# Down's first visits and the reading of its operands: other visit lengths, reads in quarters, two short visits

## The chip, the cores and the metric

The kernel runs on one core of one Trainium2 chip. The metric is the device time of one execution in microseconds; for the kernel before, the median of three runs is given. The core has five engines that this text names: TensorE (PE, with its weight loads PEld), VectorE (DVE), ScalarE (ACT), GpSimd (POOL) and SyncE (SP). Each takes its own instructions in order. Transfers are issued by SP's queue, some by POOL's and ACT's.

## The reference

One layer of an encoder on 512 tokens of width 2048, in float32: two attention mixers side by side, cross attention over 256 memory tokens, an MLP and a last norm. The change touches the MLP's second half and the norm alone:

```
hm = rmsnorm(x, g_mlp[l])
x = x + jnp.square(jax.nn.relu(hm @ w_up[l])) @ w_down[l]
return rmsnorm(x, g_final)
```

`w_up` is 2048 x 8192 and `w_down` 8192 x 2048.

## The kernel before, in words

Activations lie transposed: features on the 128 partitions, the 512 tokens along the columns. Every float32 product is three matmuls: each operand is split into a rounded part (hi) and the rest (lo), by a cast on ACT and a subtract on DVE (`hi_lo`, line 331), and hi x hi, hi x lo and lo x hi are added up in a PSUM bank. There are eight banks.

The MLP multiplies blocks of two by two with seven products in place of eight (`PRODUCTS`, named p1, q6, p7, q4, p2, q5, p3). One **unit** is one such block: a weight block of 256 x 512 against one **pair** of operands. A pair is two tiles of 128 features by 512 tokens, kept as seven sums of 256 columns, 1792 columns of hi and 1792 of lo. A unit (`strassen_pe`, line 1493) is 7 products x 2 halves x 3 matmuls of 256 columns, 42 matmuls, all on line 308.

**Up** is 16 groups `g` of 8 units; the 8 pairs of its input (`XP`) lie in the eight slots of the tile `big`. **Down** has four column groups `ng` of 512 features. Each needs 32 units, one for each of the 32 pairs that Up leaves. As only eight pairs are resident (`TP`, in the same slots of `big`), Down goes in 16 **visits** `v` of 8 units (`down_units`, line 1692): visit `v` takes column group `v % 4` and the pairs `2v` to `2v + 7`, modulo 32. So the window of pairs moves by two from visit to visit, and the pairs 0 to 5 are read a second time for the last three visits (`NLOAD = 38`).

At the end of a group of Up, `gen_up_out` (line 1523) evicts the seven banks, applies relu and square and the norm's factor, forms the seven sums in the buffer `G` (columns 0 to 4095 of the tile `fb`), and stores two pairs to `tp_dram` (line 1581). `gen_load_t` (line 1605) reads a pair back on SP's queue (line 1614, 896 KB in one transfer) and splits it by `hi_lo`. It is called once in each unit of Up's last group, when that unit's slot of `XP` is done with, and after the first two units of a visit, for the slots of the two pairs that the window leaves.

At the end of a visit `gen_down_out` (line 1640) evicts its seven banks with one ACT copy and eleven DVE additions onto `CB[ng]`, which holds the residual and then the sum. It can start when the residual has been read: `gen_load_res` (line 1626), started by the first unit of Down, waits until Up's last group has been stored, since `CB[0]` and `CB[1]` lie where `G` was, and issues 16 reads (line 1635). A unit needs seven banks when its visit begins, one bank is spare, and the others come free as the eviction of the visit before goes on. In the last four visits (`v >= 12`) `gen_square` (line 1713) squares the finished tiles on ACT and adds them up on POOL (on DVE for the last), through the one buffer `ev` that `gen_down_out` also uses. `gen_out` then forms the norm and writes the output.

Weights come in a ring of four buffers. For each unit, `load_blocks` (line 1445) issues three reads on SP (lines 1461, 1463, 1465: 256, 256 and 128 KB) and one accumulating read on POOL (line 1470, 256 KB). `strassen_split` (line 1476) adds two sums on DVE and splits in two pieces, of 1024 and 768 columns.

What sets the order: the program is written out by hand by tasks (Python generators) and a planner that keeps a clock for each engine (`Plan`, line 72). PE's instructions are written in unit order, and between them every task whose due time has come writes its next instructions. So the order of the instructions on each engine, and of the transfers on SP's queue, follows from the planner's estimates, for example that a pair's read takes 2,500 ns on the queue and lands 3,000 ns later (line 1615).

Of the kernel before, what the change touches and what calls it, by code (L numbers as in the profile page):

```python
# [158 lines left out]
def kernel(  # L159
# [20 lines left out]
    nc = tc.nc  # L180
# [1403 lines left out]
    def up_units(g):  # L1584
        st = {}

        def pe(kk):
            def run(i):
                if g == 0 and kk == 0:
                    spawn(gen_rstd_l())  # L1590
                until(lambda: kk in XP)
                if kk == 7:
                    spawn(gen_up_out(g, st), True)
                strassen_pe(i, st, XP[kk], kk == 0, kk == 7)
                if g == 15:
                    spawn(gen_load_t(kk))
            return run

        return [Unit(w_up[g * 8 + kk], 1024, pe(kk)) for kk in range(8)]

    NLOAD = 38

    def gen_load_t(s):

        p = s % 32
        yield plan.clk["pe"]
        while ("t", p // 2) not in flag:
            yield 0  # L1610
        dst = big[:, PAIR * (s % 8) : PAIR * (s % 8) + PAIR]
        hi, lo = dst[:, 0:1792], dst[:, 1792:3584]
        src = lo.bitcast(F32)
        nc.sync.dma_start(src, tp_dram[p])
        plan.issue("dma", 2500.0, [src], [], 3000)
        yield from hi_lo(hi, lo, src)
        TP[s] = dst


    CB_OFF = (0, 2048, 9472, 11520)  # L1620
# [69 lines left out]
    keep = []  # L1690

    def down_units(v):
        ng, st = v % 4, {}
        keep.append(st)

        def pe(j):
            def run(i):
                s = 2 * v + j
                if v == 0 and j == 0:
                    spawn(gen_load_res())  # L1700
                until(lambda: s in TP)
                if j == 7:
                    if v >= 12:
                        spawn(gen_square(ng, st), True)
                    spawn(gen_down_out(ng, st), True)
                strassen_pe(i, st, TP[s], j == 0, j == 7)
                if j < 2 and s + 8 < NLOAD:
                    spawn(gen_load_t(s + 8))
            return run

        return [Unit(w_dn[down_index((2 * v + j) % 32, ng)], 1024, pe(j)) for j in range(8)]

    def gen_square(ng, st):

        order = ((1, 0), (0, 0), (1, 1), (0, 1))
        for m, t in order:
            x = CB[ng][m][t]
            while ("fin", id(st), m, t) not in flag or (ng > 0 and ("sqd", ng - 1) not in flag):
                yield 0
            yield rt(x)  # L1720
            s = (yield from take(ev if ng < 3 else sq_l))[0]
            act.activation(s, x, AF.Square)
            yield rt(s)
            acc = acc_f[:, 256 * t : 256 * t + 256]
            eng = dve if ng == 3 else pool
            if ng == 0 and m == 1:
                eng.tensor_tensor(acc, s[:, 0:256], s[:, 256:512], op=OP.add)
            else:
                for e in range(2):
                    eng.tensor_tensor(acc, acc, s[:, 256 * e : 256 * e + 256], op=OP.add)  # L1730
            if ng < 3:
                ev.put(s)
            flag.add(("sqd", ng, m, t))
        flag.add(("sqd", ng))
        if ng < 3:
            for e in range(2):
                gain_tile(ng, 0, e)
                yield 0
        else:
            spawn(gen_out(), True)  # L1740
# [120 lines left out]
    first_s = len(units)  # L1861
    for g in range(16):
        units.extend(up_units(g))
    for v in range(16):
        units.extend(down_units(v))
    for i, u in enumerate(units):
        u.buf = (i - first_s) % 2 if i >= first_s else (i - first_s) % 3
# [166 lines left out]
```

## Time and profile before

| | |
|---|---|
| median of 3 runs | 2368.63 us (2363.82 to 2376.11) |
| profiled execution | 2371.74 us |
| its span, first to last instruction | 2370.0 us |
| mean granted clock of TensorE | 0.985 |
| PE busy | 2254.0 us, 95% |
| DVE busy | 1678.8 us, 71% |
| ACT busy | 1069.8 us, 45% |
| POOL busy | 394.8 us, 17% |
| moved by transfers | 409.05 MB, mean 173 GB/s |
| pairs read back (line 1614) | 38 of 896 KB |

The profile is one execution. An engine's busy time counts its instructions, not the waits between them. Helpers record the operations of many places under one line: L139 is every operation of ACT, DVE and POOL that the planner knows, L308 every matmul of the MLP. So a group is told by its tiles: `hl` holds the split weights, `big` the pairs, `fb` everything that is float32. Of rows with an engine's order of time, each is a run of like instructions: start, length, engine, what, how many, and in brackets the idle time before it with what ended that.

### The profile page before, as it was taken

How to read it: one execution, taken by the hardware profiler on the slowest of the kernel's cores; microseconds unless marked ns; L12 is line 12 of the kernel's file. 1: busy time of each engine (PE TensorE's matmuls, PEld its weight loads, DVE VectorE, ACT ScalarE, POOL GpSimd, SP SyncE). 2: the span in 40 equal slices, each digit the busy share in tenths (PEclk: the TensorE clock that was granted, in tenths of full speed). 3: DMA queues.
4: the chain of work that ended last, by engine and by line, in shares of the span. 5: the costliest groups of instructions: out<-in, count | busy, mean ns of one | idle time of the engine just before them, and what ended most of it. 6: DMA issues, size and time to landing. Idle time of an engine off the chain costs nothing.

```text
span 2370.0 us, 41508 instructions
## 1 busy us (share of the span) xinstructions
PE 2254.0 (95%) x16024; PEld 2165.4 (91%) x16024; DVE 1678.8 (71%) x2620; ACT 1069.8 (45%) x1487; POOL 394.8 (17%) x482
## 2 busy tenths in 40 slices
PE   8999999999999999899999999997799999999995
PEld 8999999998888887899999999997799999999995
DVE  7678543448734567887777878787578787777886
ACT  6543333345533455544545444455244444444442
POOL 3110100122012102211111111111111111111232
PEclk9999999999999999999999999999899999999997
DMA  5322222231243434778888888889877887878773
GB/s 173 101 85 94 69 78 81 65 107 45 89 169 101 157 126 151 184 200 238 206 235 221 230 236 212 246 223 287 257 211 201 238 218 210 221 197 240 202 193 107
DMA packets 259142, 409.05 MB, mean 173 GB/s; under 512 B 22112, under 2 KB 157296, under 8 KB 258688
## 3 DMA queue, kind: packets, MB, share of 16 engines
q1 hardware_dynamic: 220224, 337.58, 44.0%
q0 software_dynamic: 36944, 67.21, 17.0%
q8 instruction: 125, 2.05, 0.3%
q10 hardware_dynamic: 1776, 1.62, 0.2%
q14 instruction: 73, 0.60, 0.1%
HBM read 368.57 MB, written 37.75 MB: 171 GB/s over the span
## 4 chain that ended last, share of the span: by engine, by line
PE 67%; DVE 14%; DMA 9%; issue 6%; POOL 2%; ACT 1%; SPq 1%; DVEq 0%; POOLq 0%; ACTq 0%
PE bank L308 34%; PE bank L303 31%; DVE fb L139 7%; DVE hl L139 5%; DMA fb<-in_w_up_dram 5%; DMA fb<-in_w_dn_dram 2%; DMA big<-tp_dram 2%; DVE big L139 2%; PE bank L328 2%; POOL fb L139 2%; ACT hl L139 1%; ACT big L139 0%; DMA tp_dram<-fb 0%; SPq L1463 0%; DMA fb<-xs_dram 0%
## 5 line engine op out<-in xcount | busy, mean ns | idle before, releaser
L308 PE MATMUL bank<-big,hl 128*128 128x256 f32 x10752 | 1318.6, 285 | 71.3 <-DVE hl L139 35.7
L308 PEld LDWEIGHTS bank<-big,hl 128*128 128x128 f32 x10752 | 1306.6, 193 | 82.8 <-DVE hl L139 41.6
L139 ACT CAST hl<-fb 128x1024 fp32r<-128x1024 f32 (+4 forms) x699 | 637.7, 928 | 947.6 <-PE bank L308 304.2
L139 DVE TENSOR_TENSOR hl<-fb,hl 128x768 fp32r<-128x768 f32 (+4 forms) x698 | 747.5, 1087 | 401.1 <-ACT hl L139 399.6
L303 PE MATMUL bank<-hl,big 128*128 128x384 f32 (+4 forms) x2916 | 525.1, 330 | 7.4 <-ACT big L139 6.3
L303 PEld LDWEIGHTS bank<-hl,big 128*128 128x128 f32 x2916 | 479.2, 189 | 18.5 <-ACT big L139 6.3
L139 DVE TENSOR_TENSOR fb<-fb 128x256 f32<-128x256 f32 (+3 forms) x779 | 399.2, 525 | 134.9 <-DMA fb<-in_w_up_dram 82.0
L303 PE MATMUL bank<-big,hl 128*128 128x512 f32 (+1 forms) x1192 | 296.1, 390 | 0.0
L139 POOL TENSOR_TENSOR fb<-fb 128x128 f32<-128x128 f32 (+5 forms) x209 | 161.9, 797 | 701.2 <-DVE fb L139 308.3
L303 PEld LDWEIGHTS bank<-big,hl 128*128 128x128 f32 x1192 | 222.2, 188 | 43.3
L1470 POOL DMA_DIRECT2D fb<-in_w_dn_dram x128 | 110.8, 866 | 578.5 <-DMA fb<-in_w_dn_dram 311.6
L1470 POOL DMA_DIRECT2D fb<-in_w_up_dram x128 | 110.9, 866 | 531.7 <-DVE fb L139 185.0
L139 DVE TENSOR_TENSOR fb<-fb,bank 128x512 f32<-128x512 f32 x208 | 139.5, 681 | 9.2 <-PE bank L303 1.3
L139 ACT ACTIVATE fb<-fb 128x512 f32<-128x512 f32 (+2 forms) x144 | 116.7, 814 | 60.6 <-DVE fb L139 38.3
L303 PE MATMUL bank<-big 128*128 128x256 f32 (+2 forms) x534 | 113.3, 327 | 2.1 <-DVE big L139 1.2
L139 DVE TENSOR_TENSOR big<-big 128x1792 fp32r<-128x1792 f32 x38 | 76.9, 2023 | 36.4 <-ACT big L139 36.4
L139 ACT CAST big<-big 128x1792 fp32r<-128x1792 f32 x38 | 64.3, 1692 | 74.6 <-DMA big<-tp_dram 74.4
L303 PEld LDWEIGHTS bank<-big 128*128 128x128 f32 x534 | 87.1, 188 | 10.1 <-DVE big L139 2.5
L139 ACT CAST big<-bank 128x512 fp32r<-128x512 f32 (+2 forms) x119 | 61.2, 540 | 56.1 <-PE bank L328 28.0
L139 DVE TENSOR_TENSOR big<-bank,big 128x512 fp32r<-128x512 f32 (+1 forms) x102 | 62.7, 642 | 25.5 <-ACT big L139 25.4
L328 PE MATMUL bank<-cs,fb 128*128 128x128 f32 x384 | 60.2, 275 | 8.9 <-POOL fb L139 3.6
L328 PEld LDWEIGHTS bank<-cs,fb 128*128 128x128 f32 x384 | 46.3, 140 | 17.2 <-POOL fb L139 5.8
(88 smaller groups left out, 705.8 us busy)
## 6 DMA issues: line engine op xcount, KB each, us to landing
fb<-in_w_up_dram SPq DMA_DIRECT2D x256, 256.0 KB, 4.8
fb<-in_w_dn_dram SPq DMA_DIRECT2D x256, 256.0 KB, 5.0
big<-tp_dram SPq DMA_DIRECT2D x38, 896.0 KB, 8.7
fb<-in_w_up_dram POOLq DMA_DIRECT2D x128, 256.0 KB, 5.9
fb<-in_w_dn_dram POOLq DMA_DIRECT2D x128, 256.0 KB, 5.3
fb<-in_w_in_dram SPq DMA_DIRECT2D x80, 384.0 KB, 3.0
tp_dram<-fb SPq DMA_DIRECT2D x32, 896.0 KB, 9.8
fb<-in_w_out_dram SPq DMA_DIRECT2D x32, 512.0 KB, 3.3
```

The lines of the kernel that those rows point to most:

```text
L139: r = fn(*args, **kw)
L303: nc.tensor.matmul(out, lhsT, rhs, start=start, stop=stop)
L308: nc.tensor.matmul(out, lhsT, rhs, start=start, stop=stop, skip_group_check=True)
L328: nc.tensor.transpose(out, in_, ident)
L1470: nc.gpsimd.dma_start(s31, src[:, 256:768], accum_op=OP.add)
```

## The change

The visits come from a table of column group, first pair and end. The first three take 4, 6 and 8 pairs, twelve of 8 pairs follow, then come visits of 4, 2 and 8 pairs. The four visits that finish a column group are 14 to 17, in the order of the groups 2, 0, 1, 3. Only the pairs 0 and 1 are read twice (34 in all). A pair is read in four transfers of 448 columns, a quarter each, in a sequence that `pace` hands out: two quarters for each unit of Up's last group, of visit 0 and of the first two units of visit 1, then one for each unit. Cast and subtract of a pair come after its fourth quarter. The planner now counts 700 ns on the queue and 6,000 ns to landing for a quarter.

```
                 strassen_pe(i, st, XP[kk], kk == 0, kk == 7)
                 if g == 15:
-                    spawn(gen_load_t(kk))
+                    pace(2)
...
-    NLOAD = 38
-
-    def gen_load_t(s):
+    VISITS = [(0, 0, 4), (1, 0, 6), (2, 0, 8)]
+    VISITS += [(v % 4, 2 * v - 4, 2 * v + 4) for v in range(3, 15)]
+    VISITS += [(0, 28, 32), (1, 30, 32), (3, 26, 34)]
+    FINAL = (14, 15, 16, 17)
+    NLOAD = 34
+    paced = [0]
+
+    def pace(n):
+        for _ in range(n):
+            if paced[0] < 4 * NLOAD:
+                spawn(gen_load_t(*divmod(paced[0], 4)))
+                paced[0] += 1
+
+    def gen_load_t(s, x):
 
         p = s % 32
         yield plan.clk["pe"]
-        while ("t", p // 2) not in flag:
+        while ("t", p // 2) not in flag or (x > 0 and ("tq", s, x - 1) not in flag):
             yield 0
...
-        nc.sync.dma_start(src, tp_dram[p])
-        plan.issue("dma", 2500.0, [src], [], 3000)
-        yield from hi_lo(hi, lo, src)
-        TP[s] = dst
+        c = part(448 * x, 448)
+        nc.sync.dma_start(src[:, c], tp_dram[p][:, c])
+        plan.issue("dma", 700.0, [src[:, c]], [], 6000)
+        flag.add(("tq", s, x))
+        if x == 3:
+            yield from hi_lo(hi, lo, src)
+            TP[s] = dst
...
     def down_units(v):
-        ng, st = v % 4, {}
+        ng, s0, s1 = VISITS[v]
+        st, n = {}, s1 - s0
         keep.append(st)
...
-                s = 2 * v + j
+                s = s0 + j
...
-                if j == 7:
-                    if v >= 12:
-                        spawn(gen_square(ng, st), True)
+                if j == n - 1:
+                    if v in FINAL:
+                        spawn(gen_square(v, ng, st), True)
                     spawn(gen_down_out(ng, st), True)
-                strassen_pe(i, st, TP[s], j == 0, j == 7)
-                if j < 2 and s + 8 < NLOAD:
-                    spawn(gen_load_t(s + 8))
+                strassen_pe(i, st, TP[s], j == 0, j == n - 1)
+                pace(2 if v == 0 or (v == 1 and j < 2) else 1)
             return run
...
-    for v in range(16):
+    for v in range(len(VISITS)):
         units.extend(down_units(v))
```

`gen_square` tests the visit where it tested the column group, so that the squares of visit 14 start the sum and those of 17 go to DVE.

## Rows read from the trace of the kernel before

**Rows 1.** The page, part 2: PE's busy tenths in 40 slices of the span.
```profile
PE   8999999999999999899999999997799999999995
```

**Rows 2.** PE in order of time, the passage from Up to Down.
```profile
1499.79 39.04 PE L308 MATMUL bank<-big,hl 128*128 128x256 f32 x324
...
1699.22 3.92 PE L308 MATMUL bank<-big,hl 128*128 128x256 f32 x20 [15.65 <-DVE fb L139]
```

**Rows 3.** Busy time in stretches: length, PE, PEld, DVE, ACT, POOL, PE clock, transfers, GB/s.
```profile
1540.00:1704.33 164.33, 133.43 (x1040) 130.93 (x1040) 122.86 (x159) 77.33 (x80) 21.64 (x25) 0.93 0.87 255
1704.33:2340.42 636.09, 610.90 (x4996) 604.33 (x4996) 501.01 (x658) 278.04 (x296) 119.00 (x137) 0.99 0.77 208
...
1599.30:1660.10 60.80, 46.77 (x339) 44.94 (x338) 48.40 (x56) 34.24 (x32) 6.92 (x8) 0.92 0.92 288
...
1863.00:1878.30 15.30, 13.79 (x114) 13.48 (x113) 14.28 (x22) 5.33 (x7) 1.73 (x2) 1.00 0.64 153
```

**Rows 4.** Waits from 1587 to 1664: in total, times, longest.
```profile
ACT big L139 <- DMA big<-tp_dram: 23.8, 8, 7.1
```

**Rows 5.** SP's queue in order of time, the passage.
```profile
1560.56 1.37 SPq L1581 DMA_DIRECT2D tp_dram<-fb  x2
...
1602.61 2.19 SPq L1581 DMA_DIRECT2D tp_dram<-fb  x2
1604.89 5.00 SPq L1614 DMA_DIRECT2D big<-tp_dram  x2
...
1662.78 1.98 SPq L1581 DMA_DIRECT2D tp_dram<-fb  x2
1664.81 19.40 SPq L1635 DMA_DIRECT2D fb<-xs_dram  x16
1684.66 0.37 SPq L1461 DMA_DIRECT2D fb<-in_w_dn_dram  x1
```

**Rows 6.** The chain that ended last, behind Up's last store: start, length, what.
```profile
1674.26 0.38 SPq L1635
...
1677.81 6.78 DMA fb<-xs_dram
...
1691.14 6.52 DMA fb<-in_w_dn_dram
```

**Rows 7.** PE in order of time, changes of visit in Down.
```profile
1790.29 39.62 PE L308 MATMUL bank<-big,hl 128*128 128x256 f32 x328 [1.51 <-DVE hl L139]
...
2172.95 41.70 PE L308 MATMUL bank<-big,hl 128*128 128x256 f32 x344 [1.24 <-DVE fb L139]
2217.14 41.12 PE L308 MATMUL bank<-big,hl 128*128 128x256 f32 x328 [2.50 <-DVE hl L139]
```

**Rows 8.** Groups by shape, 1900 to 2370: count, busy us, mean ns, idle before.
```profile
L139 DVE TENSOR_TENSOR hl<-fb,hl 128x1024 fp32r<-128x1024 f32 x81 | 101.0, 1247 | 42.5 <-ACT hl L139 41.7 <-PE bank L308 0.8
...
L139 DVE TENSOR_TENSOR hl<-fb,hl 128x768 fp32r<-128x768 f32 x81 | 78.6, 972 | 9.3 <-ACT hl L139 9.3
L139 DVE TENSOR_TENSOR fb<-fb 128x256 f32<-128x256 f32 x168 | 75.2, 448 | 10.3 <-DMA fb<-in_w_dn_dram 7.1
...
L139 DVE TENSOR_TENSOR fb<-fb,bank 128x512 f32<-128x512 f32 x77 | 51.3, 683 | 4.3
L139 DVE TENSOR_TENSOR big<-big 128x1792 fp32r<-128x1792 f32 x18 | 36.4, 2025 | 22.7 <-ACT big L139 22.7
```

**Rows 9.** DVE in order of time, second unit of a visit.
```profile
1878.31 1.23 DVE L139 TENSOR_TENSOR hl<-fb,hl 128x1024 fp32r<-128x1024 f32 x1 [0.34 <-ACT hl L139]
```

**Rows 10.** Transfers from 1720 to 2170 by line: count, KB each, median us to landing.
```profile
fb<-in_w_dn_dram SPq DMA_DIRECT2D x168, 256.0 KB, 5.0
...
big<-tp_dram SPq DMA_DIRECT2D x20, 896.0 KB, 8.0
```

**Rows 11.** The same from 1550 to 1600.
```profile
fb<-in_w_up_dram SPq DMA_DIRECT2D x20, 256.0 KB, 5.8
...
fb<-in_w_up_dram POOLq DMA_DIRECT2D x10, 256.0 KB, 6.7
```

More of the change, by code (lines that the diff above doesn't have):

```diff
@@ L1701, in run, with gen_square @@
                 until(lambda: s in TP)
-                if j == 7:
-                    if v >= 12:
-                        spawn(gen_square(ng, st), True)
+                if j == n - 1:
+                    if v in FINAL:
+                        spawn(gen_square(v, ng, st), True)
                     spawn(gen_down_out(ng, st), True)
-                strassen_pe(i, st, TP[s], j == 0, j == 7)
-                if j < 2 and s + 8 < NLOAD:
-                    spawn(gen_load_t(s + 8))
-            return run
-        return [Unit(w_dn[down_index((2 * v + j) % 32, ng)], 1024, pe(j)) for j in range(8)]
-    def gen_square(ng, st):
+                strassen_pe(i, st, TP[s], j == 0, j == n - 1)
+                pace(2 if v == 0 or (v == 1 and j < 2) else 1)
+            return run
+        return [Unit(w_dn[down_index((s0 + j) % 32, ng)], 1024, pe(j)) for j in range(n)]
+    def gen_square(v, ng, st):
         order = ((1, 0), (0, 0), (1, 1), (0, 1))
@@ L1717, in gen_square @@
             x = CB[ng][m][t]
-            while ("fin", id(st), m, t) not in flag or (ng > 0 and ("sqd", ng - 1) not in flag):
+            while ("fin", id(st), m, t) not in flag or (v != FINAL[0] and ("sqd", v - 1) not in flag):
                 yield 0
             yield rt(x)
-            s = (yield from take(ev if ng < 3 else sq_l))[0]
+            s = (yield from take(ev if v != FINAL[-1] else sq_l))[0]
             act.activation(s, x, AF.Square)
@@ L1724, in gen_square @@
             acc = acc_f[:, 256 * t : 256 * t + 256]
-            eng = dve if ng == 3 else pool
-            if ng == 0 and m == 1:
+            eng = dve if v == FINAL[-1] else pool
+            if v == FINAL[0] and m == 1:
                 eng.tensor_tensor(acc, s[:, 0:256], s[:, 256:512], op=OP.add)
@@ L1730, in gen_square @@
                     eng.tensor_tensor(acc, acc, s[:, 256 * e : 256 * e + 256], op=OP.add)
-            if ng < 3:
+            if v != FINAL[-1]:
                 ev.put(s)
-            flag.add(("sqd", ng, m, t))
-        flag.add(("sqd", ng))
-        if ng < 3:
+        flag.add(("sqd", v))
+        if v != FINAL[-1]:
             for e in range(2):
```

## The prediction

> **What bounds the kernel now.** The page first: in its forty slices TensorE (PE) is busy for nine tenths nearly throughout, with one hole of two slices at seven tenths [rows 1]. So PE is the bound except in one place, and I looked for that place in PE's order of time. In the second half of Up, 324 matmuls run in 39.04 us without a gap [rows 2]: 0.1205 us each, 5.06 us for a unit of 42. Counted at that pace, PE lost 164.33 - 1,040 x 0.1205 = 39.0 us between 1540.00 and 1704.33, around the passage from Up to Down, and 636.09 - 4,996 x 0.1205 = 34.1 us in all the rest of Down [rows 3].
>
> The 39 us have two halves. In the first, up to 1660, PE loses 60.80 - 339 x 0.1205 = 20 us; transfers are busy for 0.92 of that time and DVE for 48.4 of 60.8 us [rows 3]. Ten pairs of operands are read back there (eight by line 1596, two by line 1708), and each costs a cast on ACT and a subtract on DVE. ACT works in order and stood eight times, 23.8 us, waiting for a pair to land, with the splits of weights queued behind it [rows 4]. SP, in order too, stood 5.00 us on two pair reads whose slots were still in use, with the next weights' reads behind them [rows 5]. In the second half one thing is slow. The last group of Up stores its pairs at 1662.78; the reads of the residual (16 tiles, line 1635) go over the buffer that these stores read from, so SP stands on them for 19.40 us, and the next weights are asked for at 1684.66 only [rows 5]. The accumulating read of those weights lands at 1691.14 + 6.52 = 1697.66 [rows 6]. DVE waits for it with a sum (line 1483), the additions that free PE's banks stand behind that sum, and PE stands 15.65 us on DVE [rows 2].
>
> In the rest of Down the loss is at the change of visit: PE stops there for 1.24 to 2.50 us [rows 7], since 11 additions of 0.683 us come on top of each unit's own 2 x 0.448 + 1.247 + 0.972 = 3.12 us of DVE [rows 8]. The 4,996 matmuls hold 14 changes: 34.1 / 14 = 2.4 us each. From 2172.95 [rows 7] to 2340.42 run 1,308 matmuls with the last three changes, which have squares beside them: 167.5 - 157.6 = 9.9 us. The eleven before cost 24.2, 2.2 each.
>
> **The change, part by part.** The matmuls are the same: 18 + 96 + 14 = 128 units. So is the tail behind the last one: the last visit still has 8 units and column group 3.
>
> *Reads in the passage.* Up's last 8 units ask for 16 quarters, four pairs, in place of eight; Down's first visit asks for two more. Before the store of 1662.78 ten pairs are asked for now, six with the change: four subtracts of 2.03 us [rows 8] and 3.7 MB less, into slots that have been free for longer, so that SP stands less. What this is worth is read from that store, since everything behind it waits for it. The stores of the last three groups begin at 1560.56, 1602.61 and 1662.78 [rows 5]: 42.05 us apart, then 60.17; the last is 18.1 late. With the change two or three pairs still fall between Up's last unit and that store, up to 6 us of DVE, of which the idle fifth of DVE takes half. I put the store 3 us behind the undisturbed distance, at 1647.7, 15 earlier. Bounds: 18.1 earlier (nothing left of the delay) and 6 (two thirds left, if transfers rather than the count of pairs make it).
>
> *A new wait behind the store.* The first visit now ends with Down's fourth unit, and its eviction needs the residual (lines 1642 and 1643). The store comes about when the fifth unit begins. PE therefore runs out of banks in the fifth unit. SP stands until the stores have landed: its residual reads flow from 1674.26, store + 11.5 [rows 6]. The four tiles of column group 0 land by store + 19, an estimate from the 6.78 us of the chain's residual read [rows 6]; five more additions of 0.683 end the fifth unit at store + 22.5. Units six to nine need 20.2 us, so the tenth begins at store + 42.7. The late weights are no second loss: those of the tenth unit landed at store + 34.9, when PE would be in the eighth. Before, the tenth unit was two matmuls old at 1704.33, store + 41.5. So of the 15 us this wait takes back 1.4: **13.6 us earlier** at the tenth unit. Bounds 4.6 and 16.7.
>
> *Two more changes of visit.* Behind that point there are 16 changes, not 14. Thirteen are plain. Their gaps of 1.24 to 1.51 us [rows 7] and some 0.3 for slower matmuls beside them give 1.8; the 2.2 of now holds ACT's waits on pair reads too, which quarters, one a unit, should thin out. I take 1.8 between 1.6 and 2.6: 23.4 us, where eleven cost 24.2. The last three have squares: 9.9 us as now, and 2 more, because two of them lie two units apart: in five units DVE has 5 x 3.12 + 22 x 0.683 = 30.6 us of work for 25.3, 5.3 too much, most of which two changes at 3.3 contain already; that evictions and squares share one buffer adds to it (bounds 0 and 8). Sum 35.3 against 34.1: **1.2 us lost**; bounds 3 gained and 18 lost.
>
> *Second pair of a visit.* Its last quarter is asked for at the change itself, and its subtract of 2.03 us falls on the second unit of the next visit. DVE has been full for 14.28 of the 15.30 us up to there [rows 3], but at 1878.31, in that unit, it waits for ACT again [rows 9]. I cost the subtract at nothing; the cover is the time between that moment and the next split's due time. If that cover is gone, it costs its 2.03 us at each change.
>
> *Fewer reads in all.* 34 pairs, not 38: 8 us of DVE beside other work; nothing.
>
> *Smaller transfers.* 136 issues on SP in place of 38, one a unit. A 256 KB read lands after 5.0 us, an 896 KB one after 8.0 [rows 10]; were the landings one after another, a pair would need 20 us, not 8, but it has ten units, 50 us, until its use. And they are not one after another: between 1550 and 1600, 30 reads of 256 KB with medians of 5.8 and 6.7 us, 183 us of landings, took place within 50 [rows 11]. I cost them at nothing. The Trainium skill speaks against the quarters: "DMA: Bandwidth & Descriptors", section "Anatomy of one DMA", gives each transfer, on GpSimd's path, a fixed 2.0 us beside its bytes; by its figures a pair costs an estimated 10.1 us in quarters and 4.1 in one piece, 6 us more a pair if nothing overlapped, which the landings between 1550 and 1600 do not bear out.
>
> Sum: 13.6 - 1.2 = 12.4 us earlier. The profiled execution took 2371.7 us (its span 2370.0), 3.1 above the median of 2368.6; on the median that is **2356.2 us**, 0.5% faster. Half a per cent, 11.8 us, is about what a measurement of this kernel can tell from no change; the forecast lies on that line.
>
> **The rivals.**
> 1. *Slower: the second pair's subtract lands in the crowded change.* For it, DVE's 15 full us there; against it, the wait of 1878.31. Price: 13 changes x 2.03 = 26 us, so 2382.6. It decides from 1.9 us a change on (24 us make 0.5% slower). Chance 0.12.
> 2. *No gain: the store comes as late as now.* If the transfers at 0.92, not the pairs on ACT and DVE, set its time, two quarters a unit keep it late: 2356.2 + 13.6 = 2369.8. Chance 0.14.
> 3. *More gain: stores and residual land sooner behind a thinner stream.* If SP's 19.40 us are halved, 2346.5. For it, they share the engines with pairs and weights; against it, the last pair read is asked for in the second unit of Down now, well before the store, and SP stood all the same. Chance 0.15.
> 4. *Slower: the transfers become the bound.* 98 more transfers are 490 us of landings at 5.0; overlapped 183 / 50 = 3.7 times, 132 us on 636 that are busy to 0.77 [rows 3]: 0.98, above the 0.92 at which PE lost 20 us of 60.8. If a seventh of Down ran at that loss, 30 us: 2386. Against it, weights of 256 KB make up most of that 0.77 already, and their landings overlap. Chance 0.04. The rule of the Trainium skill named above, a fixed cost for each transfer, is this rival's.
> 5. *It does nothing:* the quarters still come in a burst, because SP issues them in order behind its waits. 2368. Chance 0.03.
>
> **How the numbers follow.** The forecast has 0.52. Its bounds at the passage and half of those behind it give 2350 to 2370 as its own range; 0.30 of it is faster by more than 0.5%, 0.22 within. With rival 3, faster 0.45; with rivals 2 and 5, same 0.39; rivals 1 and 4, slower 0.16. The range reaches below rival 3 by half of the forecast's spread, holds rival 2, and leaves out rivals 1 and 4: 2342 to 2376.
>
> **What would show it.** Right: the store of Up's last group 42 to 50 us behind the one before, not 60; hardly a PE gap in Up's last units; one stop of some 17 us in Down's fifth unit, released by DVE, and none in the tenth; changes of 1.5 to 2 us through Down, three of 3 to 5 at the end; 34 subtracts of 1792 columns. Wrong: a store still 60 us behind (rivals 2 and 5), plain changes of over 3 us with such a subtract inside them (rival 1), a stop of under 10 us behind the store (rival 3), transfers above 0.9 in the middle of Down with DVE waiting for weights (rival 4).

## The result, and the profile after

| | before | after |
|---|---|---|
| median | 2369.20 us (8 runs, 2362.90 to 2376.11) | 2352.26 us (8 runs, 2348.78 to 2353.70) |
| profiled execution | 2371.74 us | 2348.78 us |
| PE busy | 2254.0 us, 95% | 2251.2 us, 96% |

The ratio is 0.9929, 95% interval 0.9913 to 0.9946: 16.9 us, 0.7% faster. The two profiled executions lie further apart, by 22.96 us, because that of before is 2.5 us above its median and that of after 3.5 below. So of the differences that follow some 6 us are the spread of single executions; 3.35 of it lies in Up, ahead of anything that the change touches.

The page of after: PE's slices (part 2), two groups of part 5 (count | busy us, mean ns | idle before), and one row of part 6 (count, KB, median us to landing).

```profile
PE   8999999999999999899999999999699999999985
...
L139 ACT CAST big<-big 128x1792 fp32r<-128x1792 f32 x34 | 57.5, 1691 | 59.9 <-DMA big<-tp_dram 54.8
...
L139 DVE TENSOR_TENSOR big<-big 128x1792 fp32r<-128x1792 f32 x34 | 68.7, 2021 | 3.8 <-ACT big L139 3.6
...
big<-tp_dram SPq DMA_DIRECT2D x136, 224.0 KB, 5.5
```

The hole of two slices [rows 1] is now one slice, a little deeper. There are 34 casts and subtracts, of the same length as before.

To see where the 23 us lie, I compare the same units, numbered through Up and Down: 128 is Down's first, 255 the last. Here are three stretches in the windows of PE's matmuls of the MLP alone (length, busy time, granted clock, share of transfers, GB/s), cut at the starts of the units 119, 137 and 234 and at the end of 255; first before, then after.

```profile
1574.10:1702.74 128.64, 98.93 (x759) 0.91 0.89 267
1702.74:2223.54 520.80, 498.48 (x4076) 0.99 0.80 214
2223.54:2340.42 116.88, 112.82 (x926) 1.00 0.66 174
```
```profile
1570.75:1687.99 117.24, 97.09 (x758) 0.90 0.94 272
1687.99:2190.52 502.53, 495.21 (x4077) 1.00 0.83 223
2190.52:2317.60 127.08, 115.03 (x926) 0.97 0.58 149
```

The passage gave 128.64 - 117.24 = 11.4 us, the long middle of Down 18.3, and the end took back 10.2. With the 3.35 of Up and 0.15 of the tail that is 23.0.

**The passage.** SP's queue after:

```profile
1597.61 1.40 SPq L1581 DMA_DIRECT2D tp_dram<-fb  x2
...
1644.00 1.64 SPq L1581 DMA_DIRECT2D tp_dram<-fb  x2
1646.37 20.33 SPq L1649 DMA_DIRECT2D fb<-xs_dram  x16
1668.82 0.37 SPq L1461 DMA_DIRECT2D fb<-in_w_dn_dram  x1
```

The last store of Up comes 46.39 us after the one before it, where it came after 60.17 [rows 5]. SP stands on the residual for 20.33 us, as it did for 19.40, and on two reads of pairs for 5.00 us (at 1599.05), as it did before [rows 5]. PE in the same stretch:

```profile
1604.51 31.97 PE L308 MATMUL bank<-big,hl 128*128 128x256 f32 x252 [3.03 <-DVE hl L139]
...
1642.99 0.97 PE L308 MATMUL bank<-big,hl 128*128 128x256 f32 x6 [0.17 <-ACT fb L139]
1659.20 1.65 PE L308 MATMUL bank<-big,hl 128*128 128x256 f32 x6 [15.24 <-DVE fb L139]
1661.90 35.99 PE L308 MATMUL bank<-big,hl 128*128 128x256 f32 x270 [1.04 <-DVE fb L139]
```

One gap of 3.03 us is left in Up's last group, whose eight units lost 4.9 us where they lost 10.1 (the table below). The one large stop is in Down's fifth unit, which began at 1641.94, and DVE releases it; the tenth, which began at 1687.99, has none. DVE's own row says what it stood on, the residual, no longer the late weights:

```profile
1657.66 0.69 DVE L139 TENSOR_TENSOR fb<-fb 128x512 f32<-128x512 f32 x1 [8.80 <-DMA fb<-xs_dram]
```

ACT's waits for pairs from 1587 to 1664 are half of those of [rows 4]:

```profile
ACT big L139 <- DMA big<-tp_dram: 11.9, 3, 6.2
```

**The middle of Down.** PE in order of time after: from one change of visit to the next it runs without a stop, and each change costs the same small gap, where [rows 7] have 1.24 to 2.50.

```profile
1740.60 40.89 PE L308 MATMUL bank<-big,hl 128*128 128x256 f32 x336 [0.45 <-DVE fb L139]
1781.94 40.89 PE L308 MATMUL bank<-big,hl 128*128 128x256 f32 x336 [0.46 <-DVE fb L139]
```

A unit in which PE never stops takes 5.04 us from its first matmul to the next unit's. Against that, the unit of a change is 0.71 us longer and the second unit after it 0.32: 1.03 a change, from the second to the twelfth of the thirteen plain ones.

**The end.** The change into the last visit, PE after:

```profile
2268.48 0.97 PE L308 MATMUL bank<-big,hl 128*128 128x256 f32 x6 [0.47 <-ACT fb L139]
2270.03 0.98 PE L308 MATMUL bank<-big,hl 128*128 128x256 f32 x6 [0.58 <-DVE fb L139]
2272.22 0.98 PE L308 MATMUL bank<-big,hl 128*128 128x256 f32 x6 [1.21 <-DVE fb L139]
2273.83 0.47 PE L308 MATMUL bank<-big,hl 128*128 128x256 f32 x2 [0.63 <-DVE fb L139]
2278.93 38.69 PE L308 MATMUL bank<-big,hl 128*128 128x256 f32 x310 [4.63 <-DVE hl L139]
```

This unit (248) lost 10.02 us. The copy that starts the eviction stands on ACT behind the squares of visit 15, and ACT waited three times, 6.7 us, for POOL, which was still adding squares out of the one buffer that both use; ACT in order of time:

```profile
2261.52 0.63 ACT L139 ACTIVATE fb<-fb 128x512 f32<-128x512 f32 x1 [2.57 <-POOL fb L139]
2264.38 0.63 ACT L139 ACTIVATE fb<-fb 128x512 f32<-128x512 f32 x1 [2.23 <-POOL fb L139]
...
2267.84 0.58 ACT L139 COPY fb<-bank 128x512 f32<-128x512 f32 x1 [1.89 <-POOL fb L139]
```

**Why the middle became faster** is to be read on DVE, in the order of its instructions at a change. First before (the last unit of the visit began at 1820.39), then after (at 1771.97):

```profile
1821.38 0.96 DVE L139 TENSOR_TENSOR hl<-fb,hl 128x768 fp32r<-128x768 f32 x1 [0.72 <-ACT hl L139]
1822.26 1.48 DVE L139 TENSOR_TENSOR fb<-fb 128x256 f32<-128x256 f32 x3
1823.84 0.69 DVE L139 TENSOR_TENSOR fb<-fb,bank 128x512 f32<-128x512 f32 x1
```
```profile
1772.15 0.88 DVE L139 TENSOR_TENSOR fb<-fb 128x256 f32<-128x256 f32 x2
1772.96 0.96 DVE L139 TENSOR_TENSOR hl<-fb,hl 128x768 fp32r<-128x768 f32 x1
1773.84 0.69 DVE L139 TENSOR_TENSOR fb<-fb 128x512 f32<-128x512 f32 x1
...
1785.05 2.02 DVE L139 TENSOR_TENSOR big<-big 128x1792 fp32r<-128x1792 f32 x1
```

The eviction's 11 additions, which free PE's banks, are those of 512 columns. Before, DVE waits 0.72 us for ACT ahead of the split of 768 columns, and two weight sums of 256 columns follow before the first addition (the row of three, 1.48 us, is those two and one addition). After, the two sums stand ahead of the split, in the time of that wait. So the additions begin 1.87 us after the unit's start and not some 2.7. The pair's subtract of 2.02 us stands behind all eleven, 13.1 us after the unit's start.

In the kernel before, changes of this kind, which lose 1.50 us, take turns with another kind. There (last unit from 1862.21, say) the first addition is on time, but the two sums stand among the additions, and the split of 1024 columns that the second unit of the new visit waits for stands behind all eleven, 10.9 us after the unit's start:

```profile
1873.09 2.09 DVE L139 TENSOR_TENSOR hl<-fb,hl 128x1024 fp32r<-128x1024 f32 x2
```

PE's stop for it is like the 1.51 us "<-DVE hl" of [rows 7], and this kind loses 0.16 + 1.77 us. In the kernel after, that split stands ahead of the last three additions, 7.5 us after the unit's start.

### The profile page after: what moved, and what is told of

It is laid out like the page before. It is cut to its first block, busy times and chain, and to the rows that moved or that the text cites. A ratio compares the mean times of both kernels' runs of the same rounds, so it can differ in the third digit from the quotient of the medians.

```text
span 2347.0 us, 41699 instructions
## 1 busy us (share of the span) xinstructions
PE 2251.2 (96%) x16024; PEld 2162.2 (92%) x16024; DVE 1685.3 (72%) x2638; ACT 1070.2 (46%) x1485; POOL 396.3 (17%) x482
## 4 chain that ended last, share of the span: by engine, by line
PE 68%; DVE 15%; DMA 7%; issue 6%; POOL 2%; ACT 2%; SPq 0%; DVEq 0%; POOLq 0%; ACTq 0%
PE bank L308 35%; PE bank L303 31%; DVE fb L139 8%; DVE hl L139 5%; DMA fb<-in_w_up_dram 4%; DVE big L139 2%; POOL fb L139 2%; PE bank L328 2%; DMA fb<-in_w_dn_dram 1%; ACT hl L139 1%; DMA tp_dram<-fb 1%; ACT fb L139 0%; DMA big<-tp_dram 0%; DMA fb<-xs_dram 0%; DMA fb<-in_xT_dram 0%
## 5 line engine op out<-in xcount | busy, mean ns | idle before, releaser
L139 DVE TENSOR_TENSOR fb<-fb 128x256 f32<-128x256 f32 (+3 forms) x787 | 404.7, 525 | 127.5 <-DMA fb<-in_w_up_dram 78.0
L139 DVE TENSOR_TENSOR fb<-fb,bank 128x512 f32<-128x512 f32 x222 | 149.6, 683 | 10.8 <-PE bank L303 1.3
L303 PEld LDWEIGHTS bank<-big 128*128 128x128 f32 x534 | 87.1, 188 | 10.1 <-DVE big L139 2.5
L139 ACT CAST big<-big 128x1792 fp32r<-128x1792 f32 x34 | 57.5, 1691 | 59.9 <-DMA big<-tp_dram 54.8
L139 DVE TENSOR_TENSOR big<-big 128x1792 fp32r<-128x1792 f32 x34 | 68.7, 2021 | 3.8 <-ACT big L139 3.6
```

What stands on the lines that cost most here:

```text
L139: r = fn(*args, **kw)
L303: nc.tensor.matmul(out, lhsT, rhs, start=start, stop=stop)
```

## The experiments

What was open: the change does four things at once. It reads quarters, it lays out other visits, it spaces the reads, and it tells the planner another time to landing. Which of them gives the 18 us in the middle, and which the 11 in the passage? And what do the stop in the fifth unit and the end cost? Twelve kernels ran, in four sets, each set beside the kernel before on one chip. All ratios are to that. The losses in the table are of the profiled execution: length of the stretch less 5.04 us a unit. Where the stop of the passage reaches unit 137, it stands in the column 137 to 233: 12.1 us in e1 and 6.8 in e6.

| kernel | median us | ratio, 95% | Up's last 8 units | 128 to 136 | 137 to 233 | 234 to 255 |
|---|---|---|---|---|---|---|
| before | 2369.20 | | 10.1 | 27.8 | 31.9 | 6.0 |
| after | 2352.26 | 0.9929 (0.9913 to 0.9946) | 4.9 | 21.7 | 13.7 | 16.2 |
| e1_quarters_old_visits | 2353.71 | 0.9925 (0.9908 to 0.9941) | 8.4 | 13.1 | 24.3 | 12.4 |
| e2_whole_new_visits | 2387.06 | 1.0065 (1.0046 to 1.0085) | 4.9 | 29.3 | 42.4 | 14.3 |
| e3_residual_early | 2348.17 | 0.9899 (0.9879 to 0.9919) | 4.1 | 12.4 | 18.0 | 15.8 |
| e5_squares_later | 2343.46 | one run | 1.7 | 23.6 | 14.8 | 8.4 |
| e6_before_late_estimate | 2354.59 | 0.9932 (0.9911 to 0.9953) | 4.3 | 27.2 | 16.0 | 6.7 |
| e7_quarters_early_estimate | 2370.11 | 1.0002 (0.9984 to 1.0019) | 6.4 | 30.8 | 21.7 | 13.7 |
| e8_residual_spread | 2335.62 | 0.9851 (0.9818 to 0.9884) | 3.1 | 12.8 | 14.0 | 8.4 |
| e9_old_visits_spread | 2341.36 | 0.9876 (0.9844 to 0.9909) | 4.7 | 14.9 | 14.4 | 12.5 |
| e10_whole_new_visits_late | 2386.52 | 1.0068 (1.0048 to 1.0088) | 0.3 | 33.2 | 49.1 | 17.6 |
| e11_spread_later_estimate | 2330.17 | 0.9833 (0.9819 to 0.9848) | 0.5 | 12.9 | 13.0 | 6.9 |
| e12_before_late_residual | 2341.98 | 0.9878 (0.9860 to 0.9897) | 5.4 | 18.4 | 15.7 | 5.9 |
| e13_ten_unit_visit | 2335.09 | 0.9855 (0.9830 to 0.9881) | 3.8 | 12.5 | 11.7 | 11.2 |

### One part alone: quarters, or visits

**e1_quarters_old_visits** reads quarters in the 16 old visits: four of them a unit in Up's last group, then one a unit.

```diff
-                    pace(2)
+                    pace(4)
...
-    VISITS = [(0, 0, 4), (1, 0, 6), (2, 0, 8)]
-    VISITS += [(v % 4, 2 * v - 4, 2 * v + 4) for v in range(3, 15)]
-    VISITS += [(0, 28, 32), (1, 30, 32), (3, 26, 34)]
-    FINAL = (14, 15, 16, 17)
-    NLOAD = 34
+    VISITS = [(v % 4, 2 * v, 2 * v + 8) for v in range(16)]
+    FINAL = (12, 13, 14, 15)
+    NLOAD = 38
...
-                pace(2 if v == 0 or (v == 1 and j < 2) else 1)
+                pace(1)
```

> Reads in quarters alone: the 16 visits of 8 units of the kernel before (38 pairs), four quarters a unit in Up's last group, one a unit in Down. If the passage is paid for by the number of pairs handled before Up's last store (theory), it stays as before: the last two stores some 57 to 61 us apart, about 39 us lost between Up's end and Down's tenth unit; the plain changes of visit fall from 2.2 us to about 1.0 if the quarters are what made them cheaper, so about 2357 us. Rival: bursts, not counts, made the passage dear; then the stores come 50 us apart or less and the time is near 2345. Rival: the changes got cheaper by the visits' new places, not by the quarters; then they stay at 2 us and the time is 2366 to 2370.

Measured: 0.9925, all that the change gives, without its visits. The changes in the middle cost 0.70 + 0.32, as after. The passage keeps a late store (55.18 us behind the one before) and its stop, in Down's tenth unit (137):

```profile
1706.28 38.63 PE L308 MATMUL bank<-big,hl 128*128 128x256 f32 x304 [10.31 <-DVE hl L139]
```

**e2_whole_new_visits** has the new visits and reads each pair whole, when its first quarter was due, with the old estimate.

```diff
-                spawn(gen_load_t(*divmod(paced[0], 4)))
+                if paced[0] % 4 == 0:
+                    spawn(gen_load_t(paced[0] // 4))
...
-        nc.sync.dma_start(src[:, c], tp_dram[p][:, c])
-        plan.issue("dma", 700.0, [src[:, c]], [], 6000)
+        nc.sync.dma_start(src, tp_dram[p])
+        plan.issue("dma", 2500.0, [src], [], 3000)
```

> The new visits with each pair read in one transfer, asked for where its first quarter was (with the planner's old estimate of a read). Theory: the passage is gained (stores 45 to 49 us apart, one stop of about 16 us in Down's fifth unit), the plain changes are back at about 2 us and the units with a read in them lose up to 1.4 us: about 2365 us. Rival, quarters do nothing for the changes: 2352. Rival, the passage needs the quarters too: stores 55 us apart or more and 2370.

Measured: 1.0065, slower than before and outside all that was expected. Most changes in the middle lose 3 to 4.5 us, counting the unit behind. There the subtract of a pair stands ahead of the additions, and DVE often waits for weights besides (26.1 us between 1710 and 2160, where before has 8.5). DVE at a change whose last unit began at 1787.89; the first addition comes 4.2 us after that, not 1.9:

```profile
1785.72 0.89 DVE L139 TENSOR_TENSOR fb<-fb 128x256 f32<-128x256 f32 x2 [2.60 <-DMA fb<-in_w_dn_dram]
...
1787.39 2.02 DVE L139 TENSOR_TENSOR big<-big 128x1792 fp32r<-128x1792 f32 x1
...
1792.12 0.68 DVE L139 TENSOR_TENSOR fb<-fb 128x512 f32<-128x512 f32 x1
```

How the loss divides between the two wasn't tried. So the new visits with whole reads do harm. In the passage, over the units 120 to 137, the loss is 39.4 us before, 33.6 in e1, 34.1 in e2 and 26.5 after: each of the two kernels takes off 5 to 6, and the whole change 12.9.

### The stop in the fifth unit

**e3_residual_early** takes away the wait for the residual. Column group 0 is laid over Up's eviction buffer in place of the stores' buffer, and its four tiles are read as soon as Up's last squares are done; group 1 follows the stores, the rest comes 14 us later.

```diff
             act.activation(d, four(src), AF.Square)
+            if t == 1:
+                flag.add(("ct", g))
...
-    CB_OFF = (0, 2048, 9472, 11520)
+    CB_OFF = (11520, 9472, 0, 2048)
...
-        while ("t", 15) not in flag:
+        while ("ct", 15) not in flag:
             yield 0
         for ng in range(4):
+            while ng == 1 and ("t", 15) not in flag:
+                yield 0
+            if ng == 2:
+                yield plan.clk["pe"] + 14000.0
```

> The changed kernel, with the residual and sums of column group 0 at columns 11520 to 13567 of the float32 tile and those of group 1 at 9472 to 11519, where Up's last stores read nothing; group 0 is read when Up's last group has been squared, groups 2 and 3 some 14 us after. Theory: the stop of 15.2 us and the 5 us behind it in Down's fifth unit are the wait for the residual behind the stores; they fall under 3 us, and the time to about 2335 us. Rival: with that wait gone, DVE's work of the passage or the late weights stop PE within the next five units for as long: 2345 to 2352.

Measured: 0.9899, 2348.17 us, the time of the rival (the profiled execution, 2341.87 us, is 6.3 below the median, so the losses in the table are on the low side), and the fifth unit's loss fell from 20.5 us to 3.9. Part of that came back in the next units. The sixth lost 6.41, behind a pair that ACT waits for (some 3 of it at the lower clock: the 220 matmuls below need 26.4 us at 0.12), and the eleventh 5.19, since the eight reads of the groups 2 and 3 stand on SP ahead of weights. PE, ACT and SP in order of time:

```profile
1654.57 29.36 PE L308 MATMUL bank<-big,hl 128*128 128x256 f32 x220 [3.44 <-DVE hl L139]
...
1650.08 1.69 ACT L139 CAST big<-big 128x1792 fp32r<-128x1792 f32 x1 [5.09 <-DMA big<-tp_dram]
...
1661.55 5.41 SPq L1655 DMA_DIRECT2D fb<-xs_dram  x8
```

### The end

**e5_squares_later** lets the squares of visit 15 wait until visit 16's eviction has put the shared buffer `ev` back.

```diff
         ev.put(e)
+        flag.add(("eput", id(st)))
...
         order = ((1, 0), (0, 0), (1, 1), (0, 1))
+        while v == FINAL[1] and ("eput", id(keep[FINAL[2]])) not in flag:
+            yield 0
```

> The changed kernel; the squares of the four-unit visit (15) wait until the two-unit visit's eviction has handed back the buffer that both use. If the shared buffer makes the last change dear (10.0 us in the changed kernel), the change into the last visit falls to 6 us or less. If DVE's crowd of two evictions within five units makes it, it stays at 8 us or more.

Measured, in one run: the change into the last visit lost 2.02 us where it lost 10.02, and the stretch of the end 8.4 where it lost 16.2. In e8, which has the same edit, that change lost 2.03. So 8 of the 10 us that the end took are this one buffer, held by squares when an eviction wants it. PE after the change of visit, which now has one stop:

```profile
2271.27 10.34 PE L308 MATMUL bank<-big,hl 128*128 128x256 f32 x84 [1.76 <-DVE hl L139]
```

### The estimate alone

e1's gain left two parts that could be its cause: the quarters or the planner's time to landing. An estimate changes nothing in the program but the order in which instructions stand on their engines and queues. Two kernels part the two.

**e6_before_late_estimate** is the kernel before with one number changed.

```diff
-        plan.issue("dma", 2500.0, [src], [], 3000)
+        plan.issue("dma", 2500.0, [src], [], 7000)
```

> The kernel before with one number changed: the planner takes a pair's read to land 7,000 ns after its 2,500 on the queue, not 3,000, so that cast and subtract stand later in the order of ACT and DVE; reads stay whole. Theory A, the changes of visit got cheaper because DVE and ACT no longer stand in their order behind a pair that has not landed: DVE's wait for a pair's cast (36.4 us in all before) falls under 8, the plain changes go from 2.2 to about 1.0 to 1.4 us, about 2357 us. Theory B, the size of the transfers matters (a burst of 896 KB keeps weights back): changes stay at 2 us, 2366 to 2372.

**e7_quarters_early_estimate** is the changed kernel with one number taken back.

```diff
-        plan.issue("dma", 700.0, [src[:, c]], [], 6000)
+        plan.issue("dma", 700.0, [src[:, c]], [], 2500)
```

> The changed kernel with the planner told that a quarter lands after 2,500 ns, not 6,000 (measured: median 5.5 us from issue), so that cast and subtract of a pair are placed early. Theory A: ACT and DVE stand behind unlanded quarters again, the plain changes cost 2 us or more, about 2365 us. Theory B: the transfers stay small, so the changes stay at about 1.0 us and the time at 2352.

Measured: e6 gains as much as the whole change (0.9932), and e7 nothing (1.0002). In e6 the passage is as bad as before (38.3 us over the units 120 to 137, the store 59.40 us behind the one before), but the changes are clean, 0.71 us each, and the order on DVE at both kinds of change is that of the changed kernel:

```profile
1743.89 40.58 PE L308 MATMUL bank<-big,hl 128*128 128x256 f32 x336 [0.45 <-DVE fb L139]
```

The waits for pairs between 1710 and 2160 (total, times, longest) show what the number does. First e6, in which DVE has no wait for a pair's cast at all, then e7:

```profile
ACT big L139 <- DMA big<-tp_dram: 0.7, 2, 0.4
```
```profile
ACT big L139 <- DMA big<-tp_dram: 86.7, 22, 5.3
...
DVE big L139 <- ACT big L139: 36.3, 11, 4.1
```

Before, ACT waited 41.3 us there and DVE 26.0; after, 36.7 and 2.0. A cast that is written where the planner believes the pair landed, but where it has not, makes ACT stand, and with it all that is written behind. The expectation for e7 was near in the total (2365, measured 2370) and wrong in the place: its changes still cost 0.71 + 0.32. What it lost is in the middle of visits (0.5 to 1.7 us in one unit of most), and above all in the passage, where 37.2 us are lost from Up's last group to unit 136, as before (37.9). Its changes stay clean: all eleven waits for casts lie in the last unit but two of a visit (3.60 us in unit 151, for one, behind which the next unit loses 0.83), and at the change DVE has the order of the changed kernel, with the first addition 1.9 us after the start of the visit's last unit.

**e10_whole_new_visits_late** was to say whether the estimate alone also mends e2: whole reads, new visits, 7000 in place of 3000.

> The new visits with whole reads, as in the run that was slower than before, but the planner takes a read to land 7,000 ns after its 2,500 on the queue. If only the estimate matters (theory A), the quarters add nothing: the changes fall from 3 us to about 0.7, DVE's wait for casts under 5 us in all, and the time is that of the changed kernel, 2350 to 2356. If the smaller transfers have a share of their own, it is in the passage, where 896 KB reads keep weights back: 2358 to 2366, with the passage some 5 us dearer than the changed kernel's.

It does not: 1.0068. (Its profiled execution took 2397.99 us, 11.5 above its median, so its losses in the table are high by as much.) In the same stretch ACT's wait for pairs is gone and DVE's for casts is 2.5 us, yet changes lose 2.4 us (2.23 + 0.17) and 5.7 (2.17 + 3.53) by turns. A late estimate also writes the subtract later, and with whole reads it comes to stand ahead of the additions or in their midst. DVE at a change of the second kind, whose unit began at 1832.78:

```profile
1840.95 2.02 DVE L139 TENSOR_TENSOR big<-big 128x1792 fp32r<-128x1792 f32 x1
1842.88 2.07 DVE L139 TENSOR_TENSOR fb<-fb,bank 128x512 f32<-128x512 f32 x3
```

Three additions wait for the subtract, and PE waits for the banks that they free. Of the 3.53 us that the next unit loses some 2.6 are the clock's (last section).

So the order on DVE at a change goes with its price. The sums ahead of the additions or among them: before, 1.5 to 1.9 us. A subtract ahead of them or among them: e2 and e10, mostly 2.4 to 5.7. Neither: the changed kernel, e1, e6 and e7, 0.71 and at most 0.33 more. Waits for casts in the middle of a visit are another loss, and a smaller one: before, 26.0 us of them cost PE 3.0 (in units 173, 189, 197 and 205), in e7 36.3 us cost some 8. That the estimate sets all this is shown by e6 and e7. No run changes the order on DVE by itself, so that this order, and nothing else that moves with it, makes the price is read from the rows. Nor was a whole read tried that is asked for later.

The passage needs more than the estimate. Over the units 120 to 137, in one execution of each, the loss is 39.4 us before, 38.3 in e6 (late estimate alone), 37.2 in e7 (visits and quarters), 33.6 in e1 (quarters and late estimate), 33.5 in e10 (visits and late estimate), and 26.5 after, with all three.

### What could be had

**e8_residual_spread** joins e3 and e5, and reads the other 12 tiles of the residual one by one, some 4 us apart.

```diff
         for ng in range(4):
+            while ng == 1 and ("t", 15) not in flag:
+                yield 0
+            if ng > 0:
+                yield plan.clk["pe"] + 4000.0
...
+                    if ng > 0 and (m, t) != (1, 1):
+                        yield plan.clk["pe"] + 4000.0
```

> The changed kernel with the residual of group 0 read early (columns as in the run before), the other twelve residual reads one by one, 4 us apart, behind Up's last stores, and the squares of the four-unit visit held back. Theory: the stop in the fifth unit was the residual's wait, and the 6.4 and 5.2 us that stayed at the sixth and eleventh units when the residual was read early came from twelve reads in a row on SP with weights behind them; both go, and so does the dear last change: about 2330 us. Rival: DVE's work or the transfers in the passage hold PE anyway: 2338 to 2344.

Measured: 0.9851, 2335.62 us, between the two expectations. The eleventh unit loses 2.1 us again, not 5.2, and the end 8.4; the fifth and sixth still lose 4.70 and 5.48.

**e9_old_visits_spread** has the old visits, quarters, and the residual as in e8.

```diff
-                    pace(2)
+                    pace(3)
...
-                pace(2 if v == 0 or (v == 1 and j < 2) else 1)
+                pace(2 if v == 0 and j < 4 else 1)
```

> Quarters and the spread residual, but the 16 visits of 8 units of the kernel before (38 pairs; three quarters a unit in Up's last group, two in Down's first four units, then one). Theory: the new visits' gain is in the passage alone and they pay for it with two more changes; with the residual out of the way the old visits lose a few us more in the passage (two pairs more before Down's fifth unit) and save two changes of about 1 us and the short visits' end: within 5 us of the run with the new visits, 2328 to 2338. Rival: the first visits' need of few pairs is worth 7 us as in the runs with the residual's wait: 2340 or more.

Measured: 0.9876, 2341.36 us, the side of the rival, with 12.5 us lost at the end, where two changes of the old visits cost 4.3 each beside squares.

**e11_spread_later_estimate** is e8 with 8000 in place of 6000.

> The run with the spread residual, and the planner's landing of a quarter at 8,000 ns instead of 6,000. If the 5.5 us that are left at Down's sixth unit are ACT standing behind a pair that has not landed (5 us of wait there), they go: about 2331 us. If later casts only delay the pairs' use, or the stop is DVE's work, 2336 or more.

Measured: 0.9833 (0.9819 to 0.9848), 2330.17 us, as expected, the fastest of all and 40 us under before. The sixth unit, which lost 5.48 in e8, loses nothing; Up's last group loses 0.5; and the 0.32 behind each change is gone.

**e12_before_late_residual** is e6 with the residual as in e8: old visits, whole reads.

> The kernel before, its visits and whole reads, with the late estimate of a pair's landing (7,000 ns) and the early, spread reading of the residual. The two edits act on different stretches, so their gains add: 15 us from the changes of visit and some 15 of the 18.6 us that PE lost at Down's ninth and tenth units: 2338 to 2342. If new visits and quarters carry a gain of their own in the passage, this stays 8 us or more behind the best run (2330). If the residual's place matters only with short first visits: 2350 or more.

Measured: 0.9878, 2341.98 us. Both expectations hold: the gains add, and it stays 11.8 us behind e11. Three small edits to the kernel before give 29 us; visits, quarters and later squares together add some 11 us once the rest is in order. Quarters alone add nothing to that: e9, with the old visits, has 0.9876.

**e13_ten_unit_visit** is e11 without the wait for `ev`, with a visit of ten units for group 1 at the end, and so 17 visits.

```diff
-    VISITS += [(v % 4, 2 * v - 4, 2 * v + 4) for v in range(3, 15)]
-    VISITS += [(0, 28, 32), (1, 30, 32), (3, 26, 34)]
-    FINAL = (14, 15, 16, 17)
+    VISITS += [(v % 4, 2 * v - 4, 2 * v + 4) for v in range(3, 13)]
+    VISITS += [(1, 22, 32), (2, 24, 32), (0, 28, 32), (3, 26, 34)]
+    FINAL = (13, 14, 15, 16)
...
-                pace(2 if v == 0 or (v == 1 and j < 2) else 1)
+                pace((2 if j < 4 else 0) if v == 13 else 2 if v == 0 or (v == 1 and j < 2) else 1)
```

> The best run (2330) with the two-unit visit folded into the visit before it of the same column group, which then has ten units: 17 visits, one change fewer, no evictions two units apart. If a change and the crowded end cost what they show (3 to 4 us at the last two changes), about 2327 us; if the ten-unit visit's two reads a unit cost as much, 2330 to 2333.

Measured: 0.9855, 2335.09 us, above both expectations, no better than e8 and 5 us behind e11. The middle, with one change less, loses 1.3 us less, and the end 4.3 more; how much of that is the missing wait for `ev` wasn't tried.

## Why the prediction was right, and where not

The predicted 2356.2 us stands 3.9 above the measured median, within the range. The sign is right too: the gain of 0.7% is on the far side of the half per cent on which the forecast lay. That the sum came out so near is in part luck: it put the plain changes some 8 us too dear, the gain of the passage 2.2 us too high and the last three changes 2.6 too cheap, and what made the changes cheap had no place in it.

**The passage: right.** The store was put 45.1 us behind the one before; it came at 46.39. PE's stop was put into Down's fifth unit, with DVE's additions behind the residual as its releaser; it is there, and the fifth unit ends at store + 23.5 (1667.50) for 22.5. The late weights were to be no second loss, and are none. The tenth unit was to begin at store + 42.7 and began at + 44.0. The gain of 13.6 was 11.4. A part of the working was luck, though. The prediction gave the whole gain to four pairs fewer and freer slots, and read it from the store, "since everything behind it waits for it". SP stood its 5.00 us all the same. e7 has the four pairs fewer and a store after 49.41 us, and yet loses as much as before by unit 136 (37.2 us, 37.9); e10 has its store after 46.17 us and loses 33.5.

**The term that was missing: the planner's time to landing.** The forecast walks through visits, quarters, waits and issues, and gives the new estimate, 6000 where there was 3000, not a word of cost or gain. By e6 and e7 it is worth 0.7%, as much as the whole change, with or without the rest. And the rest, quarters and visits together, comes to nothing when the estimate is held late or early: 0.9932 without them and 0.9929 with them at a late one, 1 and 1.0002 at an early one (the two late ones are 1.5 and 1.2 us behind the median landings of 8.0 and 5.5 us, the early ones 2.5 and 2.3 ahead). They aren't idle, though. The new visits with whole reads cost 0.7% (e2, e10), so quarters are what makes these visits bearable; and what the two give in the passage, the end takes back; where the wait for the residual and that for the buffer are gone as well, they are worth some 0.45% (e11 beside e12, the later squares included).

**"Thirteen are plain ... I take 1.8": too high.** They cost 1.03 (the first 2.3, the last 1.5), 15.2 us in all where 23.4 were put. The step went wrong in its reason: it put what 2.2 holds beyond 1.8 down to ACT's waits for pairs, "which quarters, one a unit, should thin out". ACT's waits were hardly thinned, 41.3 us before and 36.7 after. What changed is the order on DVE: no sum ahead of the additions or among them, and the next unit's split ahead of the last three.

**The last three changes: too low.** Predicted 9.9 + 2 = 11.9; measured 0.71 + 2.32 + 1.49 + 10.02 = 14.5. The shared buffer was named, bounded by 8, and taken at next to nothing; e5 gives it 8 by itself. The rest of Down behind unit 137, put at 1.2 lost, was 18.3 - 10.2 = 8.1 gained, outside its bound of 3 gained.

**The second pair of a visit: right, by a cover that was named wrongly.** The subtract falls into the second unit of the next visit and costs next to nothing: the 0.32 us behind each change. It stands on DVE just ahead of the split of 1024 columns that the third unit waits for; in e11, which writes it 1.1 us behind the start of that split, the 0.32 is gone. But the idle moment of [rows 9] isn't what protects it; the order is, and that is the planner's.

**The rivals.** Rival 1, the subtract in the crowded change, is real and didn't occur: e2 and e10 have it. Its price was too low. In e10 a pair of changes loses 8.1 us where after loses 2 x 1.03, that is 3.0 a change more, not 2.03; some 1.3 of it is the lower clock, which the price left out. Rival 2 did not hold: the store came early, with transfers busy for 0.97 of the time between the last two stores. Rival 3 did not: the stream was no thinner (282 GB/s between the last two stores, 277 before), and SP stood 20.33 us all the same; but e3 and e8 show that its prize was there, behind another layout. Rival 4 did not: transfers are at 0.83 in the middle of Down, and in e1, with 152 quarters, at 0.83 from 1720 to 2220 too. The rule of the Trainium skill that spoke for it ("DMA: Bandwidth & Descriptors", "Anatomy of one DMA") gives a fixed cost to each transfer on GpSimd's path. On SP's queue a quarter does take 5.5 us to land where a whole pair took 8 [rows 10]: 672 KB more took 2.5 us longer, so by these medians most of the 5.5 isn't bytes. But the landings overlap, and e1's 152 quarters cost nothing that shows (0.9925, and 0.9932 for e6 with whole reads). Rival 5 did not: the quarters came by twos, 24 of them between 1585 and the store at 1644, and the time fell.

## What to carry to other kernels

Where a planner's estimates set the order of instructions, an estimate is a parameter of the kernel: compare it with the landings in the trace (here 8 us where it said 5.5 from the issue) and try it by itself before a larger change, since one number gave what new visits and quarters gave. At a stage's change, read the order on the engine that frees the buffers: what stands ahead of its first instruction or in the midst of them delays everything, and the same work a few microseconds later cost 0.3 us here, or nothing. When two users share one buffer, price the wait from the moment at which both want it, not from the spare time of the engines.

## What the runs showed of the hardware

A stop can cost more than its own length, by TensorE's clock. Two changes of e10, one after the other, cost their own unit the same, 2.2 us, but the next unit 0.17 and 3.53; here are the windows of the stop, its end and the time behind it, of both (length, PE's busy time, granted clock, transfers, GB/s):

```profile
1797.63:1801.55 3.92, 2.92 (x19) 1.00 0.50 77
1801.55:1804.00 2.45, 2.45 (x19) 1.00 0.00 0
...
1842.29:1844.21 1.92, 0.01 (x1) 1.00 0.19 33
1844.21:1846.14 1.93, 1.32 (x8) 0.75 0.00 0
1846.14:1852.00 5.86, 5.86 (x27) 0.50 0.55 175
```

At the first the waits came in four pieces of 0.22 to 0.55 us between groups of six matmuls, 1.2 us in all, and the clock stayed at 1.00. At the second 1.92 us came in one piece, and 0.61 soon after; the granted clock then was 0.50, the lower of its two levels (1.2 GHz), for 5.9 us, in which 27 matmuls ran where some 49 fit at 0.12 us each. The 22 that are missing, 2.6 us, are most of the 3.53 us that the next unit lost. Whether the sum of the waits or the length of one piece made the difference, these rows don't tell; e5's stop of 1.76 us, in one piece, left the clock at 1.00. In the changed kernel the fifth unit's stop of 15.24 us was followed by 0.50 as well, for 7.8 us, in which 28 matmuls of 0.12 us ran beside 1.04 us of waiting: some 3.4 of that unit's 20.5 us are the clock's and not the residual's:

```profile
1659.20:1667.00 7.80, 6.75 (x28) 0.50 0.88 283
```
